# A planner's account of time is given other durations and latencies: the same instructions, in another order

## The chip, the cores and the metric

The kernel runs on one core of a Trainium2 chip. The metric is the device time of one execution in microseconds (us), the median of several runs. Five engines work side by side, each through its own instructions in the order in which they were written down: TensorE (PE, matrix products), VectorE (DVE), ScalarE (ACT), GpSimd (POOL), and SyncE (SP), which here issues the transfers (DMA). An instruction that needs a result of another engine waits for it, and everything behind it on its own engine waits too.

## The reference

One step of a decoder with two attention branches over the same normalised input, for a prompt of 2048 tokens and 32 decode tokens (8 sequences of 4), all 1024 wide, in float32:

```python
h = rmsnorm(x, norm_gain)
# A: 8 query heads, 2 key/value heads, window 128, learned sinks
# B: 3 groups of 8 heads, (window, dilation) = (128,1), (512,4), (2048,16):
#    a query at t reads the 128 keys t - j*dilation
s = jnp.where(mask, q @ k + bias, NEG_INF)       # q, k RMS-normalised per head
m = jnp.max(s); p = jnp.exp(s - m); l = sum(p)   # A: m and l take the sink too
o = p @ v / l
# the three groups of B are combined with weights proportional to l
y = x + (merge_gates * (branch_A @ w_up_a, branch_B @ w_up_b)) @ w_out
```

Beside `y` the new rows of the key and value caches are returned. The decode tokens read the cached keys and values and the new ones.

## The kernel before

The products work on float16 pairs: each float32 operand is split into a high and a low part, and a product is three matmuls (high by high, high by low, low by high). The prompt's 2048 tokens are 16 tiles of 128. The program has these stages:

- The input is normalised and transposed (`h_all`), weights are split (`Block`), the merge gates' products run (128x416).
- Branch B, group by group in the order 3 (dilation 16), 2, 1. For each of the 16 tiles of a group PE makes three projections, q, k and v, of 24 matmuls each (`proj`). The result leaves its PSUM bank by ACT (L712, L720, L992), goes through the norm (`norm`: squares on ACT, a sum on DVE, a power on POOL, a product on DVE), is split in two parts (`split`: L307 on ACT, L310 and L312 on DVE), and is transposed by a DMA (`turn`); a key's parts are copied to a second layout (`k_turn`, L755 on DVE).
- Attention of a tile (`attend`) is two units of four heads (`unit`). A unit is: score products on PE into two banks; a predicated copy (L780) and the bias with the row maximum (L786) on DVE; four exponentials on ACT (L806); a split of the probabilities; a DMA transpose; where a tile reads two key blocks, a mask product and a subtraction on DVE (L824, L826); and the value products on PE (128x64), 12 or 24 matmuls. When both units are through, `finish` takes the tile's output out of its bank (L1004 on ACT).
- The decode tokens take a turn in each group (`sample_proj`, then `sample` as a chain beside the tiles): 72 projections of 32 tokens, which leave their bank by L720 with 32 partitions, then cached scores on DVE and cached value products on PE, whose results leave by ACT at L1246.
- Branch A in the same way with its gates and the first part of the output, then the last projections.

The order of the instructions isn't written out by hand. A class `Clock` decides it while the program is built. The products of the main stream carry a counter `now` forward, each by a cost in nanoseconds (`mm`, `cost`, `tpose`). Every other chain of instructions is a Python generator. It issues an instruction, calls `use` with the engine and an estimate of its duration, and yields the time at which its result should be there; `Clock` wakes it when `now` has reached that time, and only then is its next instruction written down. `use` adds the estimate to the engine's own account and, in the kernel before, a latency `LAT` of 110 ns. `move` does the same for a transfer: `come` is when it should have arrived. So the estimates set how many projections PE has in its program between a unit's scores and its value products. Locks (`Lock`) for banks and buffers work in the same counted time. On the chip itself the engines are held by semaphores alone; the account only fixes the order in each engine's program.

One wait is of the main stream itself. In each group, behind tile 2 (branch A: tile 1), the decode tokens' projections are driven, and before that the decode step of the group before must have ended in the account:

```python
def mid():
    ck.until(lambda: box[-1] is None or box[-1].done)
    ck.drive(sample_proj(g, box))
```

`until` moves the counter from one waiting chain to the next and lets them issue; no projection of the main stream is written down meanwhile.

Of the kernel before, what the change touches and what calls it, by code (L numbers as in the profile page):

```python
# [21 lines left out]
P = 128  # L22
# [14 lines left out]
def bucket_onehot():  # L37
    """[32, 3 * 128]: for dilations 1, 4, 16, column i marks the bucket of distance (127 - i) * dilation."""
# [42 lines left out]
class Clock:  # L81
    """Decides the order in which instructions are written down. The products of the main stream carry the
    time forward; every other chain of instructions is a generator that yields the time at which its next
    inputs should be there, by a simple account of how long each engine is taken."""

    LAT = 110
# [40 lines left out]
    def use(self, e, ns):  # L127
        self.free[e] = max(self.now, self.free[e]) + ns
        return self.free[e] + self.LAT

    def move(self, ap, size=4, turned=False):
        """A transfer joins the queue; `come` is the time at which the latest one should have arrived."""
# [3 lines left out]
        self.sp = max(self.sp, self.now) + (1175 if turned else 475)  # L136
        self.queue = max(self.queue, self.sp + (100 if turned else 650)) + max(450, n / (292 if turned else 358))
        self.come = self.queue + 900
# [13 lines left out]
def hybrid_kernel(ctx, tc, xp, xs, ca, cb1, cb2, cb3, rel_bias, norm_gain, w_in, qga, kga, sinks, qgb, kgb,  # L152
# [6 lines left out]
    class SP:  # L159
# [5 lines left out]
        @staticmethod  # L165
        def turn(out, in_):
            """Transposes blocks of 128 columns in float16 on their way through the DMA."""
            nc.sync.dma_start_transpose(out=out, in_=in_)
            ck.move(out, 2, True)
# [82 lines left out]
    # time of an instruction over n elements per partition  # L252
    def ta(n, ptr=0):
        return 0.833 * n + 70 + 93 * ptr

    def tv(n):
        return n / 0.96 + 65
# [12 lines left out]
    def cost(n):  # L270
        return n / 2.4 + 0.5 if n > 64 else 27
# [8 lines left out]
    def free_bank(most):  # L280
        """The bank that was taken longest ago, with one left over where `most` says so."""
# [23 lines left out]
    def split(hi, lo, src, scale, n):  # L305
        """hi + lo = src * scale in two float16 parts."""
# [6 lines left out]
        yield use("V", tv(n))  # L313

    # ------------------------------------------------------------------ weights
    class Block:
        """Columns of a weight matrix under a power of two, split in place: the parts of chunk k are written
        over float32 words of earlier chunks."""
# [51 lines left out]
    def fetcher():  # L370
        """A block is loaded as soon as there is a place."""
# [49 lines left out]
    def last_scales():  # L421
        """The scales of the weights that come last, ahead of time, so that nothing stands between their arrival
        and their split."""
# [16 lines left out]
    def converter():  # L440
# [4 lines left out]
        for b, k in seq:  # L445
# [9 lines left out]
            use("V", tv(b.ncol))  # L455
# [11 lines left out]
    # ------------------------------------------------------------------ normalised input, transposed  # L467
# [76 lines left out]
    def first_loads():  # L544
        """The order in which the first products ask for their operands."""
# [19 lines left out]
    # where the key's place in its block lies behind the query's, the block before this one is meant  # L565
# [52 lines left out]
    # ------------------------------------------------------------------ merge gates, channel major  # L618
# [44 lines left out]
    # ------------------------------------------------------------------ attention of one tile of queries  # L663
    cv = Carve()
    sq, qn, kn = cv(512), cv(512), cv(512)
    # A head's query holds its two parts one behind the other along the contraction, its key does so in both orders.
# [41 lines left out]
    def norm(src, p0, n, nh, blk, scr, dst, gains=None, raw=None):  # L708
        """dst = per-head RMS norm of the products in src (partitions p0 to p0 + n of a bank), under gains or not;
        where dst takes the products the bank is left before scr is asked for."""  # L710
# [13 lines left out]
        yield use("V", tv(nh * 64) + 140)  # L724
        G.tensor_tensor(st[:, 2, :nh], st[:, 1, :nh], nhalf[p0:p0 + n].to_broadcast([n, nh]), op=OP.pow)  # L725
        f = use("G", 250 + 170 * nh)
# [7 lines left out]
        yield use("V", tv(nh * 64))  # L734
# [1105 lines left out]
```

## Time and profile before

| | |
|---|---|
| median of 3 runs | 2290.11 us (2286.48 to 2294.4) |
| span of the profiled execution | 2287.5 us, the only time of its own that is shown |
| mean granted PE clock | 0.963 |
| PE busy | 2047.8 us, 90% |
| DVE busy | 1533.7 us, 67% |
| ACT busy | 911.4 us, 40% |
| POOL busy | 730.8 us, 32% |

Rows of the profile name an engine, a source line, an operation, output and inputs by the program's names, and the shape. A group of instructions ends in "busy us, mean ns of one | idle time of the engine just before them <- what ended it". A row of waits gives the total in us, how often, and the longest. A row of the timeline starts with its start in the span and its duration, both in us, and has its wait in brackets at the end. A row of stages has the stretch of the span, its length, the busy time of each engine, then the granted PE clock, the DMA engines' share and GB/s. PE's records overlap a little, so the time of one matmul in a row of many is the busy time divided by the count.

### The profile page before, as it was taken

Reading aid. Unit: us, or ns where it says so; the run is one execution under the profiler, and the core shown is the slowest. Engines: PE = TensorE matmul, PEld = TensorE weight load, DVE = VectorE, ACT = ScalarE, POOL = GpSimd, SP = SyncE. Lnnn points to the kernel's source line nnn. Section 1 sums busy time; section 2 is a strip of 40 time slices with the busy share of each in tenths; the row PEclk is TensorE's granted clock in tenths of the full one; section 3 lists DMA queues with packets and bytes.
Section 4 is the critical chain, followed back from the end, with each engine's and each line's share of the span. In section 5 each row is a group of like instructions: output and inputs, shape, how many; then the busy total and the mean of one; then the engine's idle time right before and its main releaser. Section 6 shows DMA issues by size and latency. Waiting matters only on the chain. (4 is left out here: it accounts for less than half of the span.)

```text
span 2287.5 us, 36002 instructions
## 1 busy us (share of the span) xinstructions
PE 2047.8 (90%) x12998; PEld 1138.3 (50%) x12998; DVE 1533.7 (67%) x3791; ACT 911.4 (40%) x2230; POOL 730.8 (32%) x554
## 2 busy tenths in 40 slices
PE   3889999999889898899989899888788897799999
PEld 2445555566555454454444454444454455344454
DVE  4456410577756787886788888879788899732331
ACT  4523211455545554455555455643333344300100
POOL 1000000255632245452234443445635444310110
PEclk8989999999999999999999999999889999899999
DMA  4966421378769446677635555623122236233322
GB/s 151 230 201 243 164 86 53 94 167 204 200 144 270 120 121 161 153 167 213 183 83 117 120 134 129 161 72 94 39 59 68 68 94 207 75 96 120 103 86 88
DMA packets 432548, 305.31 MB, mean 133 GB/s; under 512 B 307824, under 2 KB 338064, under 8 KB 432368
## 3 DMA queue, kind: packets, MB, share of 16 engines
q1 hardware_dynamic: 432368, 303.00, 49.5%
q8 instruction: 102, 1.67, 0.3%
q14 instruction: 78, 0.64, 0.1%
HBM read 176.49 MB, written 60.36 MB: 104 GB/s over the span
## 5 line engine op out<-in xcount | busy, mean ns | idle before, releaser
L263 PE MATMUL bank<-slot,hT 128*128 128x512 f16 (+1 forms) x4992 | 1116.8, 379 | 6.4 <-ACT arena L992 3.0
L263 PEld LDWEIGHTS <-hT 128*128 128x128 f16 x4992 | 554.9, 114 | 472.8 <-issue 58.4
L263 PE MATMUL bank<-hT,slot 128*128 128x416 f16 (+4 forms) x2928 | 526.1, 343 | 18.4 <-DVE hT L310 13.9
L263 PEld LDWEIGHTS <-arena 128*128 128x128 f16 x4336 | 258.4, 100 | 329.9 <-DVE arena L826 73.6
L263 PEld LDWEIGHTS <-slot 128*128 128x128 f16 x2928 | 291.6, 100 | 249.6 <-issue 27.5
L263 PE MATMUL bank<-arena 128*128 128x64 f16 (+4 forms) x3746 | 256.9, 232 | 156.9 <-DVE arena L826 57.1
L725 POOL TENSOR_TENSOR nst<-nst,nhalf 128x8 f32<-128x8 f32 (+2 forms) x136 | 233.0, 1714 | 496.4 <-DVE nst L723 409.0
L806 ACT ACTIVATE arena<-arena,ast,inv 128x128 f32<-128x128 f32 x512 | 245.8, 482 | 97.1 <-DVE ast L794 96.8
L307 ACT ACTIVATE arena<-arena 128x512 f16<-128x512 f32 (+2 forms) x311 | 184.6, 607 | 204.6 <-DVE arena L733 100.2
L310 DVE TENSOR_TENSOR arena<-arena 128x512 f16<-128x512 f32 (+1 forms) x231 | 185.0, 810 | 45.2 <-ACT arena L307 41.1
L1165 POOL TENSOR_TENSOR arena<-arena 128x512 f32<-128x512 f32 (+1 forms) x102 | 143.1, 1403 | 152.3 <-DVE arena L1208 136.5
L390 DVE TENSOR_REDUCE amax<-slot 128x2 f32<-128x1024 f32 (+1 forms) x60 | 68.0, 1141 | 155.4 <-DMA slot<-in_w_in_dram 155.0
L263 PE MATMUL bank<-slot,arena 128*128 128x512 f16 x768 | 166.6, 379 | 0.0
L629 ACT ACTIVATE arena<-bank,wst 128x416 f32<-128x416 f32 (+2 forms) x82 | 48.4, 596 | 214.6 <-PE bank L263 200.2
L451 ACT ACTIVATE slot<-slot,gsc 128x512 f16<-128x512 f32 (+1 forms) x144 | 96.2, 681 | 88.9 <-DVE slot L454 52.3
L1699 POOL TENSOR_TENSOR arena<-arena 128x512 f32<-128x512 f32 (+2 forms) x40 | 48.7, 1218 | 239.3 <-DVE arena L1685 233.2
L712 ACT ACTIVATE arena<-bank 128x512 f32<-128x512 f32 x112 | 65.7, 591 | 146.8 <-PE bank L263 68.0
L454 DVE SCALAR_TENSOR_TENSOR slot<-slot,gsc 128x512 f16<-128x512 f32 (+1 forms) x144 | 108.0, 750 | 21.1 <-ACT slot L451 14.8
L786 DVE CUSTOM_DVE_ANT_0 arena<-bank,bias 128x128 f32<-128x128 f32 x512 | 117.1, 283 | 0.1
L307 ACT ACTIVATE arena<-arena,yk 128x512 f16<-128x512 f32 (+2 forms) x40 | 25.6, 640 | 223.8 <-POOL arena L1699 205.8
L1743 DVE SCALAR_TENSOR_TENSOR slot<-bank,ysc_t,slot 128x512 f32<-128x512 f32 (+1 forms) x33 | 24.8, 750 | 131.4 <-PE bank L263 127.0
L722 DVE TENSOR_REDUCE nst<-arena 128x8 f32<-128x512 f32 (+2 forms) x136 | 85.4, 628 | 26.0 <-ACT arena L720 25.5
(172 smaller groups left out, 1907.6 us busy)
## 6 DMA issues: line engine op xcount, KB each, us to landing
arena<-in_cache_b_kv_dram SPq DMA_DIRECT2D x144, 256.0 KB
slot<-in_w_in_dram SPq DMA_DIRECT2D x64, 512.0 KB
arena<-Qs SPq DMA_DIRECT2D x96, 256.0 KB
gates<-arena SPq DMA_DIRECT2D x78, 208.0 KB
comb<-arena SPq DMA_DIRECT2D x48, 264.0 KB
arena<-comb SPq DMA_DIRECT2D x48, 264.0 KB
arena<-gates SPq DMA_DIRECT2D x24, 512.0 KB
out_dram<-arena SPq DMA_DIRECT2D x42, 256.0 KB
```

The lines of the kernel that those rows point to most:

```text
L263: T.matmul(out, l, r, start=start, stop=stop)
L307: A.activation(hi, src, AF.Copy, scale=scale)
L310: V.tensor_tensor(lo, src, hi, op=OP.subtract)
L390: V.tensor_reduce(am[:, k:k + 2], b.rawk(k, k + 2), axis=AX.X, op=OP.max, apply_absolute_value=True)
L451: A.activation(b.part(0, k), src, AF.Copy, scale=sc)
L454: V.scalar_tensor_tensor(b.part(1, k), src, sc, b.part(0, k), op0=OP.mult, op1=OP.subtract)
L712: A.activation(dst, src, AF.Copy)
L722: V.tensor_reduce(st[:, 0, :nh], heads(s), axis=AX.X, op=OP.add)
L725: G.tensor_tensor(st[:, 2, :nh], st[:, 1, :nh], nhalf[p0:p0 + n].to_broadcast([n, nh]), op=OP.pow)
L786: V.tensor_tensor_reduce(out=sb[:, (2 * a + j) * P:(2 * a + j + 1) * P], in0=S[j][:, a, here], in1=bias[:, t.head(u, j)], scale=1.0, scala ...
L806: A.activation(e, e, AF.Exp, bias=nm[:, x:x + 1], scale=inv[:, g:g + 1], accum_out=l[:, x:x + 1])
L1165: G.tensor_tensor(sprod[:n], q, k, op=OP.mult)
```

## The change

`Clock` and the estimates take other numbers. No instruction is added, dropped or altered. The line numbers behind the class move by up to 5.

```diff
-    LAT = 110
+    LAT = 230
+    DONE = {"A": 150, "V": 245, "G": 210}
...
     def use(self, e, ns):
         self.free[e] = max(self.now, self.free[e]) + ns
-        return self.free[e] + self.LAT
+        return self.free[e] + self.DONE[e]
...
-        self.sp = max(self.sp, self.now) + (1175 if turned else 475)
+        self.sp = max(self.sp, self.now) + (1290 if turned else 475)
...
-        self.come = self.queue + 900
+        self.come = self.queue + (1500 if turned else 900)
...
     def ta(n, ptr=0):
-        return 0.833 * n + 70 + 93 * ptr
+        return 0.833 * n + 94 + 107 * ptr
+
+    def tw(n):
+        return n / 0.96 + 150

     def tv(n):
-        return n / 0.96 + 65
+        return n / 0.96 + 75
...
     def cost(n):
-        return n / 2.4 + 0.5 if n > 64 else 27
+        return n / 2.4 + 0.5 if n > 256 else n / 2.4 + 25 if n > 64 else 43
...
     # split, and the split of the weights
-        yield use("V", tv(n))
+        yield use("V", tw(n))
...
     # norm
-        yield use("V", tv(nh * 64) + 140)
+        yield use("V", 1.05 * nh * 64 + 320)
-        f = use("G", 250 + 170 * nh)
+        f = use("G", 350 + 190 * nh)
-        yield use("V", tv(nh * 64))
+        yield use("V", tw(nh * 64))
...
     # k_turn
-            e = use("V", 33 * nh + 65)
+            e = use("V", 45 * nh + 150)
...
     # unit: bias and maximum, exponential, mask, value products
-                e = use("V", tv(P) + 10)
+                e = use("V", 215)
-                f = use("A", 0.833 * P + 372)
+                f = use("A", 478)
-            use("V", tv(512))
+            use("V", 850)
-            yield use("V", tv(512))
+            yield use("V", 850)
-                    mm(o, ph, vh, n == 0, False, 27)
+                    mm(o, ph, vh, n == 0, False, 43)
```

(The other two value products change from 27 to 43 in the same way.) All line numbers of the program after are up to 5 higher: L806 becomes L811, L1004 becomes L1009, L992 becomes L997, L712 becomes L717, L720 becomes L725, L307 becomes L312, L1246 becomes L1251.

What this moves is shown at two places. The first is on ACT in group 2, around the two units of tile 7. A row with four 128x128 activations is a unit's exponentials; L1004 (L1009) is the output of the tile before leaving its bank, which stands behind that tile's last value products; L712 and L992 (L717 and L997) are projections leaving theirs. Before:

```order
L712 ACTIVATE arena<-bank_101 128x512
L720 ACTIVATE arena<-arena 128x512
L806 ACTIVATE arena,ast<-arena,ast,inv 128x128 x4
L307 ACTIVATE arena<-arena 128x512
L307 ACTIVATE arena<-arena,wst 128x512
L1004 ACTIVATE arena<-bank_108,wst 128x512
L712 ACTIVATE arena<-bank_103 128x512
L806 ACTIVATE arena,ast<-arena,ast,inv 128x128 x4
```

After:

```order
L811 ACTIVATE arena,ast<-arena,ast,inv 128x128 x4
L312 ACTIVATE arena<-arena 128x8x64
L811 ACTIVATE arena,ast<-arena,ast,inv 128x128 x4
L312 ACTIVATE arena<-arena 128x512
L717 ACTIVATE arena<-bank_102 128x512
L312 ACTIVATE arena<-arena,wst 128x512
L312 ACTIVATE arena<-arena 128x8x64
L1009 ACTIVATE arena<-bank_108,wst 128x512
L997 ACTIVATE arena<-bank_107 128x512
```

The output of tile 6, which stood between the two units' exponentials of tile 7, now stands behind both of them and behind one more projection. On PE the first unit of tile 7 had 54 projection matmuls between its scores and its value products, and has 96.

The second place is on ACT in the first tiles of group 1, where the decode tokens take their third turn. The rows with 32x512 belong to the decode tokens' projections; L1246 (L1251) takes out cached value products of the decode step of group 2. Before, from the second unit of tile 0 to the first unit of tile 1:

```order
L806 ACTIVATE arena,ast<-arena,ast,inv 128x128 x4
L307 ACTIVATE arena<-arena 128x8x64
L992 ACTIVATE arena<-bank_107 128x512
L720 ACTIVATE arena<-bank_101 32x512 x2
L1085 ACTIVATE arena<-bank_101,wst 32x512
L712 ACTIVATE arena<-bank_106 128x512
L307 ACTIVATE arena<-arena 128x512
L712 ACTIVATE arena<-bank_103 128x512
L720 ACTIVATE arena<-arena 128x512 x2
L307 ACTIVATE arena<-arena 128x512
L1004 ACTIVATE arena<-bank_108,wst 128x512
L806 ACTIVATE arena,ast<-arena,ast,inv 128x128 x4
```

After, from the same second unit of tile 0, through both units of tile 1:

```order
L811 ACTIVATE arena,ast<-arena,ast,inv 128x128 x4
L312 ACTIVATE arena<-arena 128x8x64
L997 ACTIVATE arena<-bank_103 128x512
L1251 ACTIVATE arena<-bank_106 128x512
L312 ACTIVATE arena<-arena 128x512
L811 ACTIVATE arena,ast<-arena,ast,inv 128x128 x4
L312 ACTIVATE arena<-arena 128x512 x2
L1009 ACTIVATE arena<-bank_108,wst 128x512
L811 ACTIVATE arena,ast<-arena,ast,inv 128x128 x4
L725 ACTIVATE arena<-bank_103 32x512 x2
L1090 ACTIVATE arena<-bank_103,wst 32x512
```

The decode tokens' projections, which came before the first unit of tile 1, now come behind both of its units, since a value product of the decode step of group 2 (L1251) is written down only here; between the exponentials of these three units no further q or k projection (L717) leaves a bank.

More of the change, by code (lines that the diff above doesn't have):

```diff
@@ L454, in converter @@
             V.scalar_tensor_tensor(b.part(1, k), src, sc, b.part(0, k), op0=OP.mult, op1=OP.subtract)
-            use("V", tv(b.ncol))
+            use("V", tw(b.ncol))
             b.conv = k + 1
@@ L838, in unit @@
                     vh, vl = (t.VT[y][:, s, vc:vc + 64] for y in (0, 1))
-                    mm(o, ph, vh, n == 0, False, 27)
-                    mm(o, ph, vl, False, False, 27)
-                    mm(o, pl, vh, False, n == nk - 1, 27)
+                    mm(o, ph, vh, n == 0, False, 43)
+                    mm(o, ph, vl, False, False, 43)
+                    mm(o, pl, vh, False, n == nk - 1, 43)
         PT_l[i % 2].put()
```

## The prediction

> **What bounds the kernel now.** I read the page's busy times first, then the stages, then what TensorE (PE) waits for in each. The stages are my cuts, by where the products of a group begin: start and gates, groups 3, 2 and 1 of branch B, branch A, and the last projections.
>
> ```profile
> span 2287.5 us, 36002 instructions
> PE 2047.8 (90%) x12998; PEld 1138.3 (50%) x12998; DVE 1533.7 (67%) x3791; ACT 911.4 (40%) x2230; POOL 730.8 (32%) x554
> core 0: us, PE busy (x) PEld busy (x) DVE busy (x) ACT busy (x) POOL busy (x), PEclk, DMA share, GB/s
> 0.00:441.00 441.00, 387.96 (x2154) 222.72 (x2155) 180.26 (x378) 137.03 (x227) 25.75 (x47) 0.96 0.51 155
> 441.00:799.00 358.00, 318.77 (x1973) 196.58 (x1972) 254.01 (x701) 191.54 (x478) 151.04 (x105) 0.97 0.70 181
> 799.00:1157.00 358.00, 320.95 (x2209) 174.42 (x2208) 288.48 (x745) 185.70 (x475) 137.72 (x91) 0.97 0.65 162
> 1157.00:1500.00 343.00, 318.36 (x2302) 165.94 (x2301) 286.02 (x723) 185.75 (x478) 141.20 (x95) 0.99 0.55 126
> 1500.00:1969.00 469.00, 387.74 (x2814) 228.18 (x2811) 419.50 (x1087) 184.73 (x533) 233.53 (x185) 0.92 0.31 86
> 1969.00:2287.50 318.50, 313.97 (x1556) 150.45 (x1556) 105.47 (x160) 26.67 (x40) 41.62 (x32) 0.99 0.29 96
> ```
>
> PE is the bound: it works 2047.8 of 2287.5 us, and no product is added or dropped. What can change is its idle time, 239.7 us, and its clock. By stage PE idles 53, 39, 37, 25, 81 and 5 us. The clock column says how much work ran at half rate: (1 - PEclk) times the stage gives 18, 11, 11, 3 and 38 us lost in the first five. In branch A the DVE is busy 419.5 of 469 us (89%), so there it is almost a second bound; in the groups it is busy 71 to 83%.
>
> The waits of the whole span, and PE's value products (128x64) and scores (128x128, 128x256) by stage, first group 3, then 2, 1 and A:
>
> ```profile
> PE bank L263 <- DVE arena L826: 57.1, 49, 5.0
> PE bank L267 <- DVE arena L508: 34.4, 3, 14.1
> PE bank L263 <- DVE arena L755: 32.2, 26, 4.2
> PE bank L263 <- DVE arena L824: 31.0, 15, 8.0
> PE bank L263 <- DMA arena<-arena: 26.7, 19, 5.3
> ...
> L263 PE MATMUL bank<-arena 128*128 128x128 f16 x256 | 22.4, 224 | 18.2 <-DVE arena L755 16.6 <-DMA arena<-arena 1.5
> L263 PE MATMUL bank<-arena 128*128 128x64 f16 x372 | 16.7, 197 | 16.6 <-DMA arena<-arena 14.8 <-ACT arena L720 1.8
> L263 PE MATMUL bank<-arena 128*128 128x64 f16 x660 | 27.0, 196 | 23.9 <-DVE arena L826 10.2 <-DVE arena L824 8.8 <-DMA arena<-arena 4.5
> L263 PE MATMUL bank<-arena 128*128 128x64 f16 x768 | 29.9, 194 | 19.9 <-DVE arena L826 13.7 <-DVE arena L824 4.6 <-DMA arena<-arena 1.4
> L263 PE MATMUL bank<-arena 128*128 128x64 f16 x744 | 33.5, 205 | 50.9 <-DVE arena L826 33.2 <-DVE arena L824 17.5
> ```
>
> So 111 us of PE's idle time stands before value products (16.6 + 23.9 + 19.9 + 50.9). They wait for the softmax of their unit: scores, the mask, four exponentials, a split, a transpose by DMA, then L824 and L826. PE is in order, so whatever is written down between a unit's scores and its value products is all that covers this latency. Mostly that is projections, at 1068.1 / 4608 = 0.232 us each.
>
> ```profile
> L263 PE MATMUL bank<-slot,hT 128*128 128x512 f16 x4608 | 1068.1, 387 | 5.3 <-ACT arena L992 3.0 <-ACT arena L1402 1.3 <-DVE arena L1423 0.9
> 1178.54 1.04 PE L263 MATMUL bank<-arena 128*128 128x256 f16 x8
> 1182.35 1.04 PE L263 MATMUL bank<-arena 128*128 128x256 f16 x8
> 1193.59 0.86 PE L263 MATMUL bank<-arena 128*128 128x64 f16 x24
> 1199.69 0.86 PE L263 MATMUL bank<-arena 128*128 128x64 f16 x24
> ...
> 1291.68 1.18 PE L263 MATMUL bank<-arena 128*128 128x256 f16 x8
> 1309.97 0.26 PE L263 MATMUL bank<-arena 128*128 128x64 f16 x3 [1.32 <-DVE arena L824]
> ```
>
> The first four timed rows are tile 1 of group 1: scores at 1178.54 and 1182.35, their values 15.0 and 17.3 us later, without a wait, so that the latency is at most that. The last two are the first unit of tile 7, where PE did wait: 18.3 us from scores to values.
>
> **The change, part by part.** All new numbers except those of PE only tell the account that things take longer. So a chain's next instruction is written down later, behind more projections. I counted, unit by unit, the PE work between scores and value products in the two orders, with the mean durations of the forms in the trace, and compared its growth with the wait that the trace shows before that unit's value products. A wait that is smaller than the growth goes; of a larger one the difference stays.
>
> Start. The transposes of the decode tokens (L267, 32x32) wait 12.97 us, and in the new order 48 more gate products stand ahead of them.
>
> ```profile
> 119.50 0.74 DVE L508 TENSOR_SCALAR arena<-arena,h_st 32x1024 f32<-32x1024 f32 x1 [5.38 <-POOL h_st L506]
> 120.39 0.60 PE L267 MATMUL bank<-ident,arena 32*128 32x32 f32 x4 [12.97 <-DVE arena L508]
> L263 PE MATMUL bank<-hT,slot 128*128 128x416 f16 x1872 | 335.8, 343 | 2.8 <-DMA hT<-arena 2.8
> ```
>
> 48 times 335.8 / 1872 = 8.6 us of the wait is filled with work that has to be done anyway. I take -8 (0 if those products find their own operands late, -16 if the half clock behind the wait goes too).
>
> Group 3. Work between scores and values grows from a mean of 16.5 to 19.4 us, in 31 of 32 units. Of the 16.6 us of waits the growth covers 10. The scores wait 18.2 us for the transposed query and its key copies (L755); how far these stand behind the tile before hardly changes, and I take 4 off. The half clock costs 11 us; it follows the waits, so half of it goes, 5. Sum -19 (-8 to -30).
>
> Group 2. From 20.2 to 24.2 us, in 24 of 32 units. Of 23.9 us the growth covers 18. Tiles 0 and 13 get less work than before (16.0 to 11.6 us, 22.3 to 17.1 us), which I price at +4. Scores -2, clock -5: -21 (-6 to -32).
>
> Group 1, where it turns. Before tile 3 the main stream stops until the decode step of group 2 has ended in the account; only then come the third decode projections. In the new order that step ends later in the account, and the main stream adds no projection meanwhile. Three units in a row then have 7.2, 4.1 and 6.2 us of PE work under them where there were 18.1, 16.5 and 19.1. Laid out with the latencies above, scores, wait, values, scores, wait, the place takes about 38 us for 16 us of work. PE waits 1.44 us at the same place now:
>
> ```profile
> 1173.00 0.53 PE L263 MATMUL bank<-arena 128*128 128x64 f16 x12 [1.44 <-DMA arena<-arena]
> ```
>
> So it costs +20 in waits, and +4 for the half clock behind them. The nearest ends: from the 15.0 us, 3 units times (15 - 6) = 27 us, of which two units in flight at once hide up to half, so +10 at the least; from the 18.3 us, 3 times 12, so +36. At the end of the group the last units have 13.4, 8.7 and 5.2 us instead of 19.3, 16.3 and 18.3: +9, and +3 of clock, since branch A's first projections come behind them. The other units' growth covers 10 of the 19.9 us, scores -1. Sum +25 (+8 to +45). The time that the decode step itself takes stays hidden beside the tiles: it is only the place of its projections that moves.
>
> Branch A. From 19.0 to 23.4 us, in 30 of 32 units, against 50.9 us of waits: by growth alone 48 would go, and with them some 18 of the 38 us of half clock, together -66. But the DVE has only 49.5 us of idle time in the stage, and part of that is outside its reach:
>
> ```profile
> DVE bank L780 <- PE bank L263: 12.0, 10, 2.7
> DVE arena L755 <- DMA arena<-arena: 9.1, 5, 3.8
> DVE arena L824 <- DMA arena<-arena: 5.2, 4, 1.8
> ```
>
> Moving PE's waits doesn't shorten the DVE's queue. I take -24: the DVE would then be busy 419.5 of 445 us (94%). Ends: 0, if the DVE sets the pace already, and -45, if it can be filled. I choose the middle because these 26 us of outside waits shrink only in part.
>
> The value products of the decode steps, the last projections (99% busy) and the SP and POOL queues: nothing. The same transfers are issued, in nearly the same order.
>
> Sum: -8 - 19 - 21 + 25 - 24 = -47. On the profiled 2287.5 us that is 2240.5. The median of the runs, 2290.11, is 2.6 us above this execution, so 2243.
>
> **The clock.** Below 1 the clock column comes in stretches of about 3.4 us, also behind short waits:
>
> ```profile
> 722.62 0.55 PE L263 MATMUL bank<-arena 128*128 128x128 f16 x7 [2.71 <-DVE arena L755]
> 720.50:722.60 2.10, 0.00 (x0) 0.00 (x0) 1.92 (x13) 1.47 (x3) 0.00 (x0) 1.00 0.67 241
> 723.40:726.90 3.50, 3.50 (x10) 1.35 (x9) 3.46 (x14) 2.23 (x5) 0.00 (x0) 0.51 1.01 322
> ```
>
> A wait of 2.71 us was followed, 0.8 us after PE went on, by 3.5 us at 0.51. So I count short waits as costing clock too.
>
> [...]
>
> **Rivals.** First, slower: the DVE paces the attention stages. If its queue is what ends last, later value products only move the wait to the masks' copies (L780) and the next scores. Then the gains of groups 3, 2 and A shrink to about 10 and the start's to 3, while the stall at group 1's decode turn (+25) needs no DVE to be slow: 2290 + 25 - 13 = 2302. It decides where the other terms together are below 25 us. For it speaks 89% in branch A; against it, that in groups 3 and 2 the DVE is idle 104 and 70 us while PE waits 39 and 37.
>
> Second, the sum is nil: the same waits stand elsewhere and the stall eats the rest, 2290 within 0.3% (7 us, about what a measurement of this kernel can tell from no change).
>
> Third, the full gain: latencies are shorter where PE stands still and the other engines drain, the stall costs +10, and A takes -45: -8 - 19 - 21 + 10 - 45 = -83, 2207.
>
> Fourth, short waits don't lower the clock, and the half clock in groups 3 and 2 follows something else: their two terms lose 10 and the start's and A's loses 4: 2257. [...]
>
> Fifth, the stall is larger: the decode step's plan runs so late that more than three units stand bare, +60 in group 1: 2243 + 35 = 2278 alone, and above 2297 if A gives nothing either.
>
> **How the numbers follow.** The forecast has 0.55, the full gain 0.13, the clock 0.06: faster 0.74. Same 0.09. Slower 0.17: the DVE 0.11, the larger stall with no gain in A 0.06. The range reaches from the full gain (2205) to just below the DVE's case (2300): the upper tenth lies beyond it. The forecast's own range is 2215 to 2270, by half of the terms' ends.
>
> **What would show it.** Right: waits of value products in groups 3 and 2 together fall from 40 to about 15 us, in A from 51 to 20 or more; a stall of three waits of 5 to 10 us each appears in the first tiles of group 1, with PE at half clock behind it; the transposes' wait at the start falls to about 4 us. Wrong: if the DVE's busy share in A stays at 89% with PE's waits moved to the scores, the DVE bounds; if PE's waits go but the span stays, look at the clock column; if no stall is seen in group 1, the account's delay there was not what the chip does, and the time is near the full gain.

## The result and the profile after

The changed kernel takes 2326.82 us in the median of 4 runs (2323.52 to 2331.6), against 2288.75 us for the kernel before (four runs; the 2290.11 shown ahead is of three of them): 1.0163 times as long, 95% interval 1.0145 to 1.0182. The forecast was 2243. The profiled execution of after has a span of 2329.7 us, 42.2 us more than that of before.

The profile after, its first lines and what PE waits for (us in total, times, longest):

```profile
span 2329.7 us, 36014 instructions
PE 2056.7 (88%) x12998; PEld 1142.1 (49%) x12998; DVE 1529.5 (66%) x3791; ACT 907.9 (39%) x2230; POOL 726.5 (31%) x554
...
PE bank L268 <- DVE arena L760: 34.8, 25, 4.1
PE bank L268 <- DVE arena L831: 31.4, 32, 5.1
PE bank L268 <- DMA arena<-arena: 26.9, 15, 7.0
PE bank L268 <- ACT arena L997: 26.5, 9, 6.3
PE bank L272 <- DVE arena L513: 26.3, 3, 14.1
PE bank L268 <- DVE arena L829: 26.1, 11, 9.2
PE bank L268 <- ACT arena L717: 17.1, 7, 6.3
```

The waits on the softmax's last steps fell as forecast, from 57.1 + 31.0 us (L826, L824) to 31.4 + 26.1 (now L831, L829). But two names are new: L997 and L717, ScalarE (ACT) emptying a projection's bank, together 43.6 us where L992 and L712 had 4.3 and 0.7.

To see where time went I cut both executions at the same projection matmuls, counted from the start: number 2112, 3387, 4310, 4611, 4930, 5550, 5862 and 7560, the decode tokens' own projections counted in. Behind the start, these cuts are group 3; group 2 without its end; the end of group 2; the start of group 1 with the decode turn; its middle; its end; branch A. Columns as in the rows of stages of the prediction; the counts of matmuls (x) differ where attention work moved from one stretch to the next. Before:

```profile
0.00:440.90 440.90, 387.86 (x2153) 222.65 (x2154) 180.16 (x378) 137.03 (x227) 25.75 (x47) 0.96 0.51 155
440.90:798.90 358.00, 318.77 (x1972) 196.58 (x1971) 254.11 (x701) 191.54 (x478) 151.04 (x105) 0.97 0.71 181
798.90:1062.00 263.10, 236.71 (x1680) 133.38 (x1679) 211.83 (x550) 133.84 (x357) 114.14 (x74) 0.97 0.65 151
1062.00:1157.20 95.20, 84.55 (x531) 41.19 (x530) 76.85 (x197) 51.86 (x118) 23.77 (x18) 0.96 0.67 192
1157.20:1233.90 76.70, 71.86 (x560) 37.46 (x559) 66.97 (x175) 43.95 (x113) 30.55 (x21) 1.00 0.49 99
1233.90:1409.40 175.50, 164.70 (x1193) 86.23 (x1192) 148.50 (x387) 91.42 (x244) 79.76 (x55) 1.00 0.56 129
1409.40:1499.70 90.30, 81.31 (x547) 41.89 (x546) 70.35 (x163) 50.07 (x121) 30.69 (x20) 0.96 0.58 143
1499.70:1984.60 484.90, 403.38 (x2885) 235.89 (x2884) 433.62 (x1105) 192.27 (x545) 238.17 (x188) 0.92 0.31 83
```

After:

```profile
0.00:442.20 442.20, 387.29 (x2153) 221.22 (x2154) 177.80 (x377) 136.72 (x226) 23.74 (x46) 0.95 0.52 154
442.20:824.10 381.90, 322.93 (x1960) 198.01 (x1959) 250.93 (x696) 181.33 (x463) 150.53 (x105) 0.94 0.64 168
824.10:1072.70 248.60, 233.57 (x1605) 131.21 (x1603) 202.44 (x509) 128.79 (x343) 110.39 (x73) 0.96 0.64 142
1072.70:1186.20 113.50, 86.24 (x547) 43.46 (x546) 88.69 (x240) 58.77 (x143) 23.43 (x17) 0.88 0.63 140
1186.20:1295.00 108.80, 93.28 (x665) 44.44 (x664) 71.33 (x199) 50.69 (x129) 33.06 (x22) 0.94 0.55 138
1295.00:1460.70 165.70, 160.74 (x1136) 84.30 (x1133) 147.69 (x357) 86.44 (x229) 77.24 (x51) 1.00 0.57 130
1460.70:1576.30 115.60, 86.49 (x589) 46.09 (x588) 78.15 (x211) 57.76 (x150) 36.20 (x27) 0.84 0.51 126
1576.30:2026.30 450.00, 386.64 (x2860) 229.22 (x2859) 407.15 (x1045) 177.27 (x506) 234.50 (x187) 0.95 0.34 91
```

Stretch by stretch, after less before: start +1.3, group 3 +23.9, group 2 -14.5, its end +18.3, the decode turn +32.1, middle of group 1 -9.8, its end +25.3, branch A -34.9, the rest +0.5. In the gains PE's idle time fell; in each of the four losses it rose, by 20, 17, 11 and 20 us, and the clock fell with it.

Two places show what stands there. The first is at the end of group 2. Rows of PE, ACT and SP (start, duration, wait in brackets):

```profile
1081.56 3.83 PE L268 MATMUL bank<-slot,hT 128*128 128x512 f16 x9 [6.32 <-ACT arena L997]
...
1080.91 0.60 ACT L997 ACTIVATE arena<-bank 128x512 f32<-128x512 f32 x1 [9.60 <-DMA out_dram<-arena]
...
1072.56 1.54 SPq L163 DMA_DIRECT2D slot<-in_w_in_dram  x1
...
1074.67 0.42 SPq L163 DMA_DIRECT2D out_dram<-arena  x1
```

PE waits for a free bank. ACT should empty it into the staging buffer `stV`, and stands for 9.60 us because the store of that buffer's last content, issued at 1074.67 behind weight loads, has not landed. The exponentials that stand behind L997 in ACT's program start only at 1082.40. `v_chain` and `k_rows` give the buffer back (`stV_l.put()`, `stK_l.put()`) as soon as the store is issued: the account takes the store as done at once.

The second place is the decode turn in group 1:

```profile
1189.93 3.41 PE L268 MATMUL bank<-slot,hT 128*128 128x512 f16 x15
...
1205.19 3.73 PE L268 MATMUL bank<-arena 128*32 128x512 f32 x20 [3.01 <-ACT arena L997]
...
1213.71 4.65 PE L268 MATMUL bank<-arena 128*128 128x256 f16 x28 [2.30 <-DVE ast L791]
...
1226.29 0.26 PE L268 MATMUL bank<-arena 128*128 128x64 f16 x3 [2.21 <-ACT arena L312]
...
1234.37 5.79 PE L892 MATMUL bank<-slot,hT 128*32 128x512 f16 x72
1240.09 4.06 PE L268 MATMUL bank<-slot,hT 128*128 128x512 f16 x18
```

Between the first row and the last, from 1193.3 to 1240.1 us, there is no projection of the prompt: this is the stop that the order showed, with the 72 decode projections at its end. (`MIDS`, below, is indexed by group: group 3 takes its turn behind tile 1, the other two groups and branch A behind tile 2.)

### The profile page after: what moved, and what is told of

Its sections match the earlier page's. It is cut to its first block, busy times and chain, and to the rows that moved or that the text cites. A ratio compares the mean times of both kernels' runs of the same rounds, so it can differ in the third digit from the quotient of the medians.

```text
span 2329.7 us, 36014 instructions
## 1 busy us (share of the span) xinstructions
PE 2056.7 (88%) x12998; PEld 1142.1 (49%) x12998; DVE 1529.5 (66%) x3791; ACT 907.9 (39%) x2230; POOL 726.5 (31%) x554
## 5 line engine op out<-in xcount | busy, mean ns | idle before, releaser
L730 POOL TENSOR_TENSOR nst<-nst,nhalf 128x8 f32<-128x8 f32 (+2 forms) x136 | 223.3, 1642 | 576.4 <-DVE nst L728 343.9
L268 PE MATMUL bank<-arena 128*128 128x64 f16 (+5 forms) x3746 | 265.7, 237 | 139.2 <-DVE arena L760 34.8
L811 ACT ACTIVATE arena<-arena,ast,inv 128x128 f32<-128x128 f32 x512 | 245.9, 482 | 161.2 <-DVE ast L799 161.0
L312 ACT ACTIVATE arena<-arena 128x512 f16<-128x512 f32 (+2 forms) x311 | 183.5, 606 | 165.0 <-DVE arena L738 89.2
L717 ACT ACTIVATE arena<-bank 128x512 f32<-128x512 f32 x112 | 66.1, 590 | 120.1 <-DMA out_dram<-arena 63.8
L312 ACT ACTIVATE arena<-arena,yk 128x512 f16<-128x512 f32 (+2 forms) x40 | 25.5, 638 | 207.0 <-POOL arena L1704 189.0
```

The source lines that it names most:

```text
L268: T.matmul(out, l, r, start=start, stop=stop)
L312: A.activation(hi, src, AF.Copy, scale=scale)
L717: A.activation(dst, src, AF.Copy)
L811: A.activation(e, e, AF.Exp, bias=nm[:, x:x + 1], scale=inv[:, g:g + 1], accum_out=l[:, x:x + 1])
```

## The experiments

Every ratio is to the kernel before, timed on the same chip. "Stop" is a place where the main stream waits in the account and writes no projection down: in `mid` for the decode step of the group before, or, as the end of the section on the prediction shows, in `pbank` for a free bank. Where nothing else is said, the outputs are all computed.

**Take away the first stop by moving the turn.**

```diff
-    MIDS = (2, 2, 2, 1)
+    MIDS = (2, 4, 2, 1)
```

> The kernel after, but the decode tokens of group 1 take their turn behind tile 4 instead of tile 2, when the decode step of group 2 has ended in the account too; nothing else is edited. In the order the three units that had 7, 4 and 6 us of products under their softmax have 18 to 24 again. Theory A (the main stream's stop at this turn costs what the stretch from projection 4611 to 4930 lost, 32 us, some of it half clock): about 2297 us, and the stretch takes 77 to 80 us instead of 109. Rival (the softmax there is late for want of DVE time, and what is saved is paid a tile later): no less than 2318 us.

2340.09 us, ratio 1.0204 (1.0185 to 1.0223): slower than the kernel after. The stretch itself went from 108.8 to 81.1 us, as theory A said. But the end of group 1 took 132.2 instead of 115.6 us and branch A 484.2 instead of 450.0. The rival was right about the time. In this order the decode step of group 1 starts later: its last cached value products stand at projection 5808, already among the first of branch A (after: 5775, before: 5613). The trace has a stop there, 31.3 us without a projection of the prompt from 1509.3 us, in which PE waits 15.78 us on end for the DVE's L829. In branch A all of the gain is gone. Its own turn comes later, at projection 5928, and doesn't stop in this order, so why branch A lost 34 us is not shown.

**Take away the stores, in the order of after and in the order of before.**

```diff
-            SP.dma_start(rows[:, :512], stK)
+            ck.move(rows[:, :512])
...
-                SP.dma_start(rows[:, 512:], stV)
+                ck.move(rows[:, 512:])
```

> The kernel after, with the stores of the prompt's new key and value rows of branch B left out (three outputs are not written); their transfers stay in the account, so that the order of all other instructions is that of the kernel after. Theory B (projections in groups 3 and 2 wait for a bank, because ScalarE can't empty it into the staging buffer before the store of that buffer's last content has landed): PE's waits before projections in these groups fall from 45 us to under 10, ScalarE's waits for stores (144 us there) are gone, and the time falls by 30 to 45 us to about 2290. Rival (ScalarE is late there for its own reasons, exponentials and weight splits ahead of the eviction): the waits stay under another name, the time falls by less than 8 us.

> The kernel before with the same stores left out, in its own order. Theory B says that the stores were hidden there (PE waits 3.2 us before projections in group 3 and nothing in group 2): 0 to 8 us less than 2288.75, about 2284. If the stores cost by their traffic alone, and not by who waits for them, the gain is as large as in the kernel after.

Without stores the kernel after takes 2273.84 us, 0.9907 (0.9879 to 0.9935), and the kernel before 2266.35 us, 0.9881 (0.9853 to 0.9909). So the stores cost about 58 us in the new order (1.0163 to 0.9907) and 27 us in the old one; "hidden" was wrong for before. The gain on after, 53 us by the medians, is more than the 30 to 45 that I expected. But PE's waits before projections in groups 3 and 2 fell from 45.4 to 24.3 us only, not to under 10: 15.9 of them are in group 2, where ACT is late for reasons of its own, as the rival said. Group 3 in the new order takes 333.8 us without them (row below: length, PE, PEld, DVE, ACT, POOL, clock, DMA), 48 us less than with them, and in the old order 344.7, 13 us less.

```profile
441.30:775.10 333.80, 310.01 (x1960) 195.49 (x1959) 250.13 (x693) 182.19 (x463) 150.18 (x105) 0.97 0.66 165
```

> The kernel after with both edits: the decode turn of group 1 behind tile 4, and the row stores of branch B left out. Theories A and B speak of different places, so the gains add: about 2260 us, below the kernel before. If DVE time is what is short, as the prediction's first rival said, the sum falls well short, to 2285 or more.

Both edits together: 2269.88 us, 0.9895 (0.9873 to 0.9917). By the medians the turn's edit is worth 4 us beside the missing stores (the intervals overlap), far from the 30 that were expected, and the 2285 that were to speak for the DVE were not reached either. Against the run without stores alone the turn's stretch takes 82.8 instead of 109.8 us, and the end of group 1 and branch A 9 and 26 us more: as in the first experiment, what the edit saves at its place is paid behind it.

**The wait or the traffic?** The same bytes at the same places, read from a buffer that is never written again:

```diff
-            SP.dma_start(rows[:, :512], stK)
+            SP.dma_start(rows[:, :512], hT[0][:, 0, :1024].bitcast(F32))
...
-                SP.dma_start(rows[:, 512:], stV)
+                SP.dma_start(rows[:, 512:], hT[0][:, 0, :1024].bitcast(F32))
```

> The kernel after, with the same row stores of branch B, of the same size at the same places in the queue, but read from a part of the transposed input that nothing writes again instead of from the staging buffers (the three cache outputs hold other values); every engine's order is that of the kernel after. Theory B (what costs is that the next eviction waits until the buffer's store has landed): nearly all of the gain of the kernel without stores (53 us), about 2275 to 2285. Rival (the stores cost by their bytes and their turns in the queue): less than 15 us gained, 2312 or more.

2280.79 us, 0.9934 (0.9912 to 0.9956). Of the 2.56% that leaving the stores out gains, 2.29 come back here. So the cause is the wait for the buffer; the rest, for bytes and turns in the queue, lies within the two intervals. The store doesn't wait for its own data here either, but in the kernel after SP stood only 4.2 us for that (for POOL's L975).

**Take away the stops where they arise.** The decode chains wait until the account sees an engine idle (`ck.idle`, with 150 ns of work left at most):

```diff
-    def idle(self, *engines, slack=150, most=1e9):
+    def idle(self, *engines, slack=1500, most=1e9):
```

> The kernel after, but the chains of the decode step that wait for an idle engine in the account take it as idle when 1500 ns of work are left instead of 150. In the order the decode steps of groups 2 and 1 then end before the main stream asks for them (at product 4560 and 5739 instead of 4632 and 5775), and the units at the start of group 1 have 19 to 24 us under their softmax again. Theory C (longer durations let the account see DVE and POOL busy, the decode step falls behind, and the main stream stops for it twice): the first stop's 28 us come back, and of the 25 us at the end of group 1 about half; some 2290. Rival (as when the turn was moved: the stop's cost is paid later, in branch A): 2318 or more.

2275.61 us, 0.992 (0.9902 to 0.9937): faster than before and than after, with the change as it is, and by more than the some 37 us that I expected. (The default slack also serves one call in the weights' scaling, for at most 1500 ns.) The decode turn's stretch and the end of group 1:

```profile
1177.40:1249.20 71.80, 70.43 (x553) 37.08 (x552) 58.90 (x157) 40.48 (x109) 29.33 (x19) 1.00 0.45 108
1413.70:1521.70 108.00, 88.86 (x654) 49.03 (x653) 88.50 (x228) 63.40 (x166) 36.76 (x25) 0.87 0.59 147
```

71.8 instead of 108.8 us, PE busy throughout; 108.0 instead of 115.6; branch A keeps its gain (446.2). So what cost was not the turn's place but the late decode step. Of the 25 us at the end of group 1, however, it gives back 7.6, not half.

**Parts of the account alone, on the kernel before.**

> The kernel before with only the durations of ScalarE, VectorE and GpSimd instructions changed; latencies, transfers and PE costs as before. In the order both stops are there (4, 4 and 7 us under the softmax at the start of group 1; the decode step of group 1 ends at the last product of the group) while the work under the softmax hardly grows (16.3, 20.9, 18.3 and 19.6 us on average against 16.5, 20.2, 19.4 and 19.0). Theory C: slower than before by 35 to 60 us, about 2335. Rival (the loss comes from the latencies and transfer times): within 10 us of before.

> The kernel before with only the transfer times of the account changed (1290 for 1175, and 1500 instead of 900 behind a transposing transfer). In the order there is no stop, and the work under the softmax grows to 16.9, 22.4, 21.2 and 21.3 us on average. The prediction's first step (growth covers waits before value products) by itself: 25 to 35 us less than before in groups 2, 1 and A, some lost again at the stores in group 3: about 2268. Rival (a longer distance is no gain, since the DVE paces the stages): 2288 or more.

> The kernel before with only the latencies of the account changed (230, and 150, 245 and 210 behind ScalarE, VectorE and GpSimd, for 110). No stop in the order; 17.9, 20.3, 20.1 and 18.8 us under the softmax against 16.5, 20.2, 19.4 and 19.0. By the prediction's first step a small gain, 2285 to 2292; by the rival that what counts is the longer hold of the staging buffers, a loss of 10 us or more in group 3.

Durations alone: 2361.31 us, 1.0297 (1.0274 to 1.032); both stops are there (105.1 and 117.2 us in their stretches), and the loss, 66 us by the medians, is a little more than I expected. Transfer times alone: 2326.59, 1.0138 (1.0115 to 1.0162); latencies alone: 2312.01, 1.0073 (1.005 to 1.0095). PE's own costs, the fourth part, were not run alone. The last two have no stop in `mid` and still lose. What they share is a longer wait for stores; no run takes the stores out of these two orders, so that this stays an argument. ACT's waits for them in the kernel before, then with transfer times alone, then with latencies alone:

```profile
ACT arena L712 <- DMA out_dram<-arena: 59.8, 16, 5.5
ACT arena L992 <- DMA out_dram<-arena: 39.3, 12, 8.6
...
ACT arena L717 <- DMA out_dram<-arena: 82.4, 17, 17.0
ACT arena L997 <- DMA out_dram<-arena: 74.2, 17, 14.5
...
ACT arena L717 <- DMA out_dram<-arena: 80.0, 17, 8.1
ACT arena L997 <- DMA out_dram<-arena: 71.2, 16, 8.4
```

99 us became 157 and 151 (144 in the kernel after). Group 3 lost 8 and 27 us. The ends of groups 2 and 1 lost too, 27 and 18 us with transfer times, 13 and 17 with latencies; those have few stores, and their cause is open (below). My expectation for transfer times was 58 us too low. It also holds a case against my first step: in branch A the cover grew from 19.0 to 21.3 us and waits before value products fell from 50.7 to 43.5, but others rose (those for L1338, before: L1333, from 9.0 to 17.5), and the stage took 9 us longer. For latencies the rival named the sign and the place, a loss of 10 us or more in group 3.

**Let the account know of the stores.**

```diff
             SP.dma_start(rows[:, :512], stK)
+            yield ck.come
             stK_l.put()
...
                 SP.dma_start(rows[:, 512:], stV)
-            stV_l.put()
             t.v = True
+            if rows is not None:
+                yield ck.come
+            stV_l.put()
```

> The kernel after, but the account counts the staging buffers of keys and values as taken until their store should have landed, so that the next eviction is written down behind that time. Instructions the same, order another (17.3, 20.5, 20.9 and 22.1 us under the softmax). Theory B: PE's waits before projections in groups 3 and 2 fall from 45 to under 20 us, and the time to about 2295. Rival (the bank stays full as long, whatever the account says, and PE waits for it in another place): 2318 or more.

> The kernel before, with the staging buffers counted as taken until their store should have landed. Theory B: leaving the stores out gained 27 us here, in groups 3 and 2, so that counting them may gain up to half of it: about 2283. Rival (the gain of this edit in the kernel after came from the decode turn that it moved, not from the stores): within 5 us of before.

> The kernel after with both changes of the account: staging buffers held until their store should have landed, and the slack of 1500 ns for the decode step. Theories B and C name different places, but holding the buffers alone already took the first stop out of the order, so the gains don't add in full: 2262 to 2275 us. If the place of a stop is a matter of chance in the order, no better than the better one of the two, 2276 or more.

On after: 2284.3 us, 0.9949 (0.9933 to 0.9966). On before: 2270.12 us, 0.9888 (0.9867 to 0.991), nearly all of what leaving the stores out gave; ACT's waits for them, on before:

```profile
ACT arena L712 <- DMA out_dram<-arena: 24.7, 8, 4.4
ACT arena L993 <- DMA out_dram<-arena: 5.1, 3, 3.3
```

30 us instead of 99. Of the 19 us that this run's span is shorter, 11 lie in groups 3 and 2 ahead of its end; the rest lies at the end of group 2 and the decode turn, which the new order also shortens. On after the gain has another source too: PE's waits before projections in groups 3 and 2 did not fall under 20 us as I expected (33.7 us, from 45.4), but the other order put the first stop out of the way (74.0 us in that stretch), which the expectation didn't name. Both account edits on after gave 2297.81, 1.001 (0.9997 to 1.0023), worse than either alone: group 3 took 352.9 us, but the end of group 1 124.1 and branch A 477.0 instead of 108.0 and 446.2. The last sentence of my expectation came true: the gains of these two edits don't add.

**Take away both costs, in either order.** The stores from a buffer that nothing rewrites, and the slack of 1500:

> The kernel after with both found costs taken away: the row stores of branch B read a buffer that nothing writes again (three cache outputs hold other values), and the slack is 1500 ns. If the two add: 2327 - 46 - 51 = 2230 us, with groups 3 and 2 shorter than in the kernel before and only the ends of groups still longer. If they are one cost seen twice: about 2270 us.

> The kernel before with the same two edits. Its decode step was never late in the account, so the slack should do nothing, and the stores cost 27 us by leaving them out: 2265 to 2275 us. The difference to the kernel after with both away is what the longer cover itself is worth: 35 to 45 us if the prediction's first step is right and the two costs add, near 0 if not.

After with both away: 2206.39 us, 0.9644 (0.9625 to 0.9664). Before with both away: 2272.56 us, 0.9928 (0.9907 to 0.9949). Group 3, the end of group 2, the end of group 1 and branch A, in the order of after, then of before:

```profile
437.50:767.80 330.30, 308.07 (x1961) 195.86 (x1960) 251.30 (x698) 184.50 (x466) 149.64 (x105) 0.98 0.74 193
995.10:1107.10 112.00, 95.73 (x611) 45.90 (x610) 93.73 (x268) 65.34 (x160) 28.95 (x21) 0.91 0.73 195
1343.40:1452.40 109.00, 89.02 (x653) 48.84 (x652) 86.90 (x228) 62.99 (x166) 37.09 (x25) 0.89 0.62 146
1452.40:1897.40 445.00, 385.38 (x2860) 228.92 (x2858) 399.90 (x1065) 181.04 (x519) 229.89 (x187) 0.96 0.35 92
...
436.10:784.60 348.50, 312.29 (x1972) 195.48 (x1971) 254.95 (x702) 192.51 (x478) 152.26 (x105) 0.97 0.71 185
1040.30:1134.80 94.50, 85.23 (x530) 41.31 (x529) 74.41 (x194) 51.86 (x118) 22.33 (x18) 0.96 0.70 198
1388.30:1477.70 89.40, 79.56 (x547) 41.97 (x546) 66.76 (x156) 48.47 (x119) 28.21 (x20) 0.94 0.55 133
1477.70:1968.80 491.10, 400.63 (x2885) 234.96 (x2884) 434.16 (x1108) 195.81 (x547) 238.66 (x188) 0.92 0.30 84
```

With nothing in the way the order of after is 66 us faster than that of before; I had expected 35 to 45. On after the two edits gain 120 us, more than the 97 of both alone: they are two costs, and here their gains more than add. On before they gain 16 us, where leaving the stores out gained 27; how much of the 27 is the wait is therefore not settled there. By the two spans the new order gains 18 us in group 3, 28 in group 2 without its end, 17 in the first two stretches of group 1 and 46 in branch A, and loses 37 at the two ends. Of these 17.5 and 19.6 us at the ends, 10.5 and 9.5 are more PE busy time, with 81 and 106 more matmuls: attention that lags further behind the projections and so falls into the end; the other 7 and 10 us are idle. That all of the 66 us is the worth of longer cover is not shown: branch A takes 491.1 us here and 466.0 in the last run below, in two orders made with the old estimates.

**The version that the runs point to**, on before, with nothing left out: buffers held and a slack of 1500.

> The kernel before with the staging buffers counted as taken until their store should have landed, and a slack of 1500 ns; nothing is left out. The buffers alone gave 0.9888 of before. The slack moves little in this order (18.5 instead of 19.4 us under the softmax in group 1): 2262 to 2278 us.

2258.69 us, 0.9876 (0.985 to 0.9901): faster than both kernels, a little below the expected range, and not told apart from holding the buffers alone (0.9888).

## Why the prediction was wrong, point by point

**The steps that failed** are two. "The SP and POOL queues: nothing. The same transfers are issued" put the stores at nothing: they cost 58 us in the new order and 27 in the old one, and turned group 3 from a gain into a loss. "The time that the decode step itself takes stays hidden beside the tiles" put the late decode step at its turn's place alone: taking it earlier gives 51 us by the medians.

**What bounds** held: PE waits for value products, and longer covers take part of those waits away. The step from there to the sum failed, since PE began to wait for other things. Of the signs that I had named, the waits before value products fell in groups 3 and 2 together from 40.5 to 22.9 us (named: about 15), and in branch A from 50.9 to 31.1. The stall in group 1 is there, but as many waits of at most 3.0 us and not as three of 5 to 10, and the clock was 0.83 in the stop (1195 to 1235 us) and 0.99 behind it. The transposes' wait did not fall.

**Start**, -8, measured +1.3. The transposes stand 48 products later, and waited 14.07 us instead of 12.97. Their input went along: POOL's L511 (before: L506) ran at 129.74 us instead of 118.88. I priced the products that fill the wait and not the chain that ends it, which was rewritten by the same account.

**Group 3**, -19, measured +23.9: the sign is wrong, and it is the step "the SP and POOL queues: nothing. The same transfers are issued". The same stores were issued, but the evictions that reuse their buffers came at other times relative to their landing. As I read the code, a longer account holds `stV` longer (its split waits until the tile before has its values), so that the next eviction, already due, follows the store at once; no run measures this step by itself. The profile of before had it in its rows of ACT's waits, 59.8 and 39.3 us for stores, which I did not read: I asked what PE waits for, and not what the engines wait for that must free PE's banks. With both costs away in both orders group 3 gains 18 us against the forecast's 19; without stores alone it gains 11.

**Group 2**, -21, measured -14.5 in its body and +18.3 at its end. In the body the mechanism and the size are about right. At the end PE stands before projections for 6.32, 5.51 and 6.27 us, the first of them, and the last in part, behind a store; but leaving the stores out took only 4 us off this stretch (109.5), so that most of it is something else. Without stores PE still waits there 7.02, 2.51 and 4.42 us for ACT's evictions; what makes ACT late is not shown.

**Group 1**, +25, measured +47.6. The stop was predicted by place and kind, at +24; its stretch is 32.1 us longer, 10.7 of it idle and the rest half clock (1 - 0.94 of 108.8 us) and work moved into it, and taking the late decode step away shortens it by 37.0. What I had at +12 for the end of the group was 25.3. The waits before value products that I had priced there at +9 rose by 11.7 us; the rest is other waits, 4.4 us for a bank (L1428) among them, and more work in the stretch. My working named the decode step as late in the account; it missed that work behind the turn waits for it as well, so that a delay that is moved out of one place can show at the next.

**Branch A**, -24, measured -34.9, and -46 with both costs away. The DVE term was too careful: the DVE was busy 407.2 of 450.0 us, 90% and not the 94% that I had named. It did not get fuller, it had less to do: 26 us less than in this stretch before, some of it done earlier (7.8 us more at the end of group 1) and some behind the stretch. The waits of L826 and L824 fell from 50.7 to 31.0 us.

**The rivals.** The slower case was put on the DVE as the pacing engine. It came out on that side, even above its 2302, but not by that mechanism: with both costs away in both orders the new one is 66 us faster. The second rival's words, that the same waits stand elsewhere, come nearest to the mechanism, but it named no place and put the sum at nil. The larger stall was the nearest in kind. No rival spoke of buffers that wait for a store, and that term alone is 58 us. The range's upper end, 2300, was set by the DVE's case and missed.

**The clock.** Half clock followed the waits: the stretches that lost went to 0.94, 0.88, 0.94 and 0.84, and those that gained stayed within 0.01 or rose (branch A 0.92 to 0.95). The size was not wrong by itself; it followed the wrong sign of the waits.

**In part open**: the ends of groups 2 and 1 have 4 to 28 us more PE idle time than in the kernel before in every order made with the new account or a part of it. At the end of group 1 the trace of after shows a second stop:

```profile
1538.94 1.46 PE L268 MATMUL bank<-slot,hT 128*128 128x512 f16 x6
1549.60 0.34 PE L268 MATMUL bank<-arena 128*128 128x64 f16 x3 [9.20 <-DVE arena L829]
...
1556.35 0.34 PE L268 MATMUL bank<-arena 128*128 128x64 f16 x3 [3.98 <-DVE arena L829]
...
1562.75 4.52 PE L268 MATMUL bank<-slot,hT 128*128 128x512 f16 x12 [4.37 <-DVE arena L1428]
```

No projection of the prompt runs from 1540.4 to 1562.7 us, and none for 14.0 us from 1502.8; in before the longest such stretch, from group 3 on, is 10.3 us. The 22.3 us lie at projection 5808. There the main stream waits in the account for a free bank (`pbank`), and one bank is held by branch A's first gate projection, whose eviction waits until the decode step of group 1 has ended (`ga_chain`); in the account the stop ends with that step. So the late decode step stops the main stream here too, outside `mid`. With the slack of 1500 this stretch is gone, but one of 17.7 us stands at projection 5664. What holds the banks there, and what makes the end of group 2 longer, is not shown.

## What to carry to other kernels

When a change moves instructions, look beyond what the bounding engine waits for: read also what the engine that frees its banks waits for, since the same stores cost 27 us in one order here and 58 us in the other. Here an account nearer to the trace in what it counts made worse what it doesn't count: the time that a store holds its buffer, and helper chains that yield to busy engines. Mending both at once was no gain over mending one (1.001 against 0.9949 and 0.992 on after, 0.9876 against 0.9888 on before), so test a gain by taking the suspected wait away in both orders.

## What the runs showed that was not expected

One store of 256 KB held its buffer for longer than its issue of 0.42 us suggests: issued at 1074.67 us, it let the buffer go at 1080.91, 6.2 us later, behind weight loads, with the DMA engines at a share of 1.05 from 1069 to 1081 us. Over the kernel before such waits kept ACT standing for 99 us, at 40% busy time, and leaving the stores out there gained 27 us.
